# Sixteen of the 22 row blocks of a down projection by seven block products instead of eight, on one Trainium2 core

## The chip, the cores and the metric

The kernel runs on one core of a Trainium2 chip. The metric is the device time of one execution in microseconds (us). Three runs of the kernel before took 1229.63, 1230.88 and 1231.22 us: the median is 1230.88 us. One more execution was profiled; its own time was 1229.33 us, and the span of its trace is 1227.6 us. The engines are TensorE (PE: matmuls; PEld: its weight loads), VectorE (DVE), ScalarE (ACT), GpSimd (POOL) and SyncE (SP, which only issues transfers here).

## The reference, cut to what matters

```python
x = x + merged @ w_o
hn2 = rmsnorm(x, norm2_w)
up, ffn_new = causal_dwconv(hn2 @ w_up, ffn_buf, ffn_conv_w, ffn_conv_b)
x = x + (jax.nn.silu(up[..., :D_FF]) * up[..., D_FF:]) @ w_down
```

This is the end of one decoder layer: 512 prompt tokens (and 16 meta tokens, which the down projection leaves out) and 64 tokens of running sequences, so 576 columns reach the down projection. The model width is 1024, D_FF is 2816: `w_down` has 22 row blocks of 128 rows and 8 column blocks of 128. Everything is float32. Ahead of it stand the other mixers of the layer (an input projection, a pooling mixer, a state-space scan, their merge), which the change touches only with transfers.

## The kernel before, in words

**A product.** Each float32 operand is cut into a rounded part (`wh`, `hi`) and the rest (`wl`, `lo`). `mm3` (lines 119 to 124) issues three matmuls for one 128x128 weight block: wl by hi (L122), wh by hi (L123), wh by lo (L124). The weights stand still, the tokens stream, a result has 128 output features by some 288 tokens. `load_w` loads weights through SP into `wr` (two buffers, L95); `split_w` has ACT write `wh` (L116) and DVE write `wl` (L117), each with two buffers.

**Order.** `run` (L178 on) goes through a list of units. A unit is all matmuls of one column block; after it come its `post` and then the split of the unit two places further on. A scheduler fixes each engine's order when the program is built; then every engine works strictly in order, and an instruction waits on semaphores. Tiles come from pools of a fixed number of buffers, so an instruction can also wait for a buffer.

**The feed-forward stage.** For each of the 22 blocks j there is a gate unit and a value unit of 48 matmuls. `ffn_conv` (L1152 to L1169) takes a result out of PSUM: POOL first writes the state's columns into `ext` (L1156), DVE scales the two halves into it (L1157 to L1159), POOL saves the last columns (L1161), ACT and DVE do the convolution (L1165, L1167). `gate_post` adds the tanh and its product (L1179, L1180); `val_post` multiplies by the gate (DVE, L1190), rounds (ACT, L1194) and leaves the rest to POOL (L1195).

**The down projection** (`down_units`, L1262) runs in two parts. After block 11 come 8 units over row blocks 0 to 11 (two halves of 288 tokens); after block 21 come 8 units over row blocks 12 to 21 (halves of 320 and 256 tokens), between which the finished columns are transposed and scaled for the output (`out_block`, `out_half`, L1227 to L1260). `down_post` (L1220) adds each half to the residual `x2` on DVE.

POOL issues no transfer in the kernel before. The lines that do the products and the sequence of units:

## Time and profile before

| what | value |
|---|---|
| median of three runs | 1230.88 us |
| the profiled execution, its span | 1229.33 us, 1227.6 us |
| PE busy | 1213.3 us, 99% of the span |
| DVE, ACT, POOL busy | 778.6, 554.3, 163.5 us |
| mean granted TensorE clock | 0.997 of full speed |
| moved by DMA | 144.00 MB, mean 117 GB/s |

The span is that of the trace; the execution's own time contains 1.7 us more. Matmuls are pipelined: the duration in a matmul's row is longer than the time to the next one's start, so durations must not be added up; the distance between starts counts. Rows of DVE and ACT overlap a little for the same reason. "Idle before, releaser" names what ended a wait.

### The profile page before, as it was taken

To read this page: it belongs to the slowest core of one execution; us is meant where nothing else is said; L and a number is where in the kernel's file an instruction comes from. 1 tells how busy PE (TensorE), PEld (TensorE's weight loads), DVE (VectorE), ACT (ScalarE), POOL (GpSimd) and SP (SyncE) were. 2 spreads that over 40 slices of the span, in tenths; PEclk is the share of its full clock that TensorE was granted. 3 is DMA by queue.
4 is the path that set the end of the run, shared out by engine and by line. 5 is a ranking of instruction groups with operands and counts; after the bars stand their busy time and mean duration, and the time that the engine had idled before them with its cause. 6 is when DMAs were issued, how large, how long until landed. Compare 5 with 4: busy or idle time off the path is not lost.

```text
span 1227.6 us, 22630 instructions
## 1 busy us (share of the span) xinstructions
PE 1213.3 (99%) x9159; PEld 1176.5 (96%) x9159; DVE 778.6 (63%) x1378; ACT 554.3 (45%) x1167; POOL 163.5 (13%) x323
## 2 busy tenths in 40 slices
PE   9999999999999999999999999999999999999996
PEld 7999999999999999989999999999999999999996
DVE  6785246668997998886643443477666235667634
ACT  6444443555757567655532223443443112433432
POOL 0340000012012013021100001221212000121100
PEclk9999999999999999999999999999999999999998
DMA  7144425653554545664454432123222223222322
GB/s 213 50 137 128 134 89 181 174 161 80 155 146 124 155 135 154 184 168 118 134 154 123 143 131 98 41 91 96 90 70 78 78 86 104 70 69 91 112 70 77
DMA packets 173432, 144.00 MB, mean 117 GB/s; under 512 B 11622, under 2 KB 162830, under 8 KB 173321
## 3 DMA queue, kind: packets, MB, share of 16 engines
q1 hardware_dynamic: 172865, 142.14, 39.5%
q8 instruction: 72, 1.18, 0.4%
q10 hardware_dynamic: 464, 0.42, 0.1%
q14 instruction: 31, 0.25, 0.1%
HBM read 122.43 MB, written 20.34 MB: 116 GB/s over the span
## 4 chain that ended last, share of the span: by engine, by line
PE 94%; DVE 3%; DMA 1%; issue 1%; ACT 1%; POOL 0%; SPq 0%; DVEq 0%; ACTq 0%; POOLq 0%
PE mm L122 28%; PE mm L123 27%; PE mm L124 27%; PE px L765 2%; PE px L827 1%; PE px L787 1%; PE px L796 1%; PE px L749 1%; DMA wr<-in_w_in_dram 1%; PE px L840 1%; DVE wl L117 1%; PE px L880 1%; PE px L739 0%; DVE ext L561 0%; PE px L122 0%
## 5 line engine op out<-in xcount | busy, mean ns | idle before, releaser
L122 PE MATMUL mm<-s,wl 128*128 128x288 f32 (+4 forms) x2512 | 753.1, 300 | 0.6 <-DVE wl L117 0.6
L123 PE MATMUL mm<-s,wh 128*128 128x288 f32 (+4 forms) x2512 | 746.2, 297 | 0.0
L124 PE MATMUL mm<-s,wh 128*128 128x288 f32 (+4 forms) x2256 | 670.7, 297 | 0.0
L122 PEld LDWEIGHTS mm<-s,wl 128*128 128x128 f32 x2512 | 473.4, 188 | 9.2 <-issue 6.5
L123 PEld LDWEIGHTS mm<-s,wh 128*128 128x128 f32 x2512 | 473.1, 188 | 2.9 <-issue 2.4
L124 PEld LDWEIGHTS mm<-s,wh 128*128 128x128 f32 x2256 | 424.1, 188 | 1.4 <-issue 1.4
L117 DVE TENSOR_TENSOR wl<-wr,wh 128x1024 fp32r<-128x1024 f32 (+1 forms) x164 | 198.2, 1208 | 173.1 <-ACT wh L116 172.7
L116 ACT ACTIVATE wh<-wr 128x1024 fp32r<-128x1024 f32 (+1 forms) x164 | 170.1, 1037 | 236.2 <-PE mm L124 199.0
L124 PE MATMUL mm<-t,wh 128*128 128x290 f32 (+1 forms) x256 | 76.0, 297 | 0.0
L1167 DVE SCALAR_TENSOR_TENSOR acc<-ext,ffT,acc 128x592 f32<-128x592 f32 x88 | 74.2, 844 | 1.7 <-ACT acc L1165 0.2
L663 DVE SCALAR_TENSOR_TENSOR acc<-ext,scT,acc 128x616 f32<-128x616 f32 x72 | 63.8, 887 | 0.4
L737 ACT ACTIVATE t<-t,TK 128x128 f32<-128x128 f32 (+1 forms) x160 | 49.0, 385 | 25.5 <-DVE t L735 25.5
L952 POOL TENSOR_TENSOR sqs<-sqs,acc 128x578 f32<-128x578 f32 x19 | 32.2, 1697 | 142.2 <-ACT acc L951 77.3
L124 PEld LDWEIGHTS mm<-t,wh 128*128 128x128 f32 x256 | 48.2, 188 | 0.0
L1194 ACT ACTIVATE s<-ext 128x512 fp32r<-128x512 f32 (+1 forms) x44 | 17.1, 436 | 64.3 <-DVE ext L1190 64.3
L1158 DVE TENSOR_TENSOR ext<-mm,t 128x224 f32<-128x224 f32 x43 | 16.8, 391 | 41.7 <-PE mm L124 41.7
L1195 POOL TENSOR_TENSOR s<-ext,s 128x512 fp32r<-128x512 f32 (+1 forms) x44 | 37.4, 871 | 34.7 <-ACT s L1194 34.7
L1220 DVE TENSOR_TENSOR t<-t,mm 128x288 f32<-128x288 f32 (+2 forms) x30 | 13.6, 452 | 44.1 <-PE mm L124 43.9
L884 ACT ACTIVATE t<-t,spr 128x128 f32<-128x128 f32 x128 | 40.3, 394 | 1.1 <-PE px L827 1.0
L806 POOL TENSOR_TENSOR s<-s,tmp 128x256 f32<-128x256 f32 (+1 forms) x32 | 31.9, 1018 | 66.9 <-DVE tmp L800 59.1
L1165 ACT ACTIVATE acc<-ext,ffT 128x592 f32<-128x592 f32 x44 | 38.2, 870 | 1.6 <-DVE ext L1159 1.6
L1161 POOL COPY t<-ext 128x18 f32<-128x18 f32 x44 | 11.3, 258 | 203.1 <-DVE ext L1159 203.0
(292 smaller groups left out, 1288.0 us busy)
## 6 DMA issues: line engine op xcount, KB each, us to landing
wr<-in_w_in_dram SPq DMA_DIRECT2D x29, 1024.0 KB
wr<-in_w_up_dram SPq DMA_DIRECT2D x22, 1024.0 KB
t<-in_state_ssm_dram SPq DMA_DIRECT2D x32, 256.0 KB
t<-cumD SPq DMA_DIRECT2D x16, 512.0 KB
out_dram<-t SPq DMA_DIRECT2D x32, 256.0 KB
wr<-in_w_ssd_out_dram SPq DMA_DIRECT2D x8, 1024.0 KB
wr<-in_w_down_dram SPq DMA_DIRECT2D x8, 768.0 KB
wr<-in_w_down_dram SPq DMA_DIRECT2D x8, 640.0 KB
```

Source lines behind the costliest of these rows:

```text
L116: S.activation(wh[:, :kb, :n], wr, AF.Copy)
L117: V.tensor_tensor(wl[:, :kb, :n], wr, f(wh[:, :kb, :n]), ALU.subtract)
L122: PE.matmul(o, wl[:, k, :m], hi[:, a:b], start=first, stop=False)
L123: PE.matmul(o, wh[:, k, :m], hi[:, a:b], start=False, stop=False)
L124: PE.matmul(o, wh[:, k, :m], lo[:, a:b], start=False, stop=last)
L663: V.scalar_tensor_tensor(acc[:, 0:616], ext[:, k:k + 616], scT[:, kb, 24 + k:25 + k], acc[:, 0:616], op0=ALU.mult, op1=ALU.add)
L737: S.activation(seg[:q, h, :q], seg[:q, h, :q], AF.Exp, scale=-1.0, bias=sums_[:, h:h + 1])
L884: S.activation(v[:, b], v[:, b], AF.Copy, scale=elS[:, 4 * u + 2 * i + b, 4 * g + j:4 * g + j + 1])
L952: G.tensor_tensor(sums[key], sums[key], t[:, :NA], ALU.add)
L1165: S.activation(acc[:, 0:w], ext[:, 0:w], AF.Identity, scale=ffT[:, kb, 16:17], bias=ffT[:, kb, 19:20])
L1167: V.scalar_tensor_tensor(acc[:, 0:w], ext[:, k:k + w], ffT[:, kb, 16 + k:17 + k], acc[:, 0:w], op0=ALU.mult, op1=ALU.add)
L1195: G.tensor_tensor(l, a, f(h), ALU.subtract)
```

## The change: what it does

Row blocks 0 to 15 are taken in two groups of 8. In a group, the weights are seen as a 2x2 arrangement: A11, A12, A21, A22 (the first index: which half of the 1024 output columns; the second: even or odd row blocks). The gated activations are seen as B11, B12, B21, B22 (even or odd row blocks; which 288 tokens). In place of the 8 products A by B the kernel computes 7, with sums of the A and of the B as operands (the table `SEVEN`). Row blocks 16 to 21 stay as they were, in units of 6 row blocks.

The sums S1 to S4 of weights (1 MB each and group) are built in device memory by transfers: a plain copy, issued by ACT, and then one to three additions into it, issued by POOL (`accum_op=add`). There are 8 copies and 14 additions in all. `held_back` ties each to an earlier weight split, and `placed` spreads them over the merge, the output projection, and the feed-forward with the products in it. Weights of the products come in tiles of four products (`Parts`, 1 MB, four transfers); a unit `Two` is two products of 4 weight blocks and one half each, 24 matmuls. The operands N1, N2, T3, T4 are made by DVE in `val_post`. `seven_post` adds each product to up to three places of `x2`. Also, `rs2` moves to another pool, and `ff_states` two units later.

```diff
-        S.activation(wh[:, :kb, :n], wr, AF.Copy)
-        V.tensor_tensor(wl[:, :kb, :n], wr, f(wh[:, :kb, :n]), ALU.subtract)
+        round_done.append(S.activation(wh[:, :kb, :n], wr, AF.Copy))
+        split_done.append(V.tensor_tensor(wl[:, :kb, :n], wr, f(wh[:, :kb, :n]), ALU.subtract))
...
+    SEVEN = (("A11", "B11"), ("A12", "B21"), ("S4", "B22"), ("S2", "N2"), ("S1", "N1"), ("S3", "T3"), ("A22", "T4"))
...
+            rows = src[k0 * 128:(k0 + 8) * 128, :].rearrange("(k e p) c -> e k p c", e=2, p=128)
+            self.at = {f"A{i + 1}{e + 1}": rows[e][:, :, 512 * i:512 * i + 512] for i in range(2) for e in range(2)}
+            self.d = {s: dp.tile([4, 128, 512], F32, name=f"{name}{s}") for s in ("S1", "S2", "S3", "S4")}
...
+            return lambda: held_back(S.dma_start(out=self.d[s], in_=self.at[a]), round_done[-1], mybir.DependencyClass.NoSync)
...
+            return lambda: held_back(G.dma_start(out=self.d[s], in_=self.at[a], accum_op=ALU.add), split_done[-3], mybir.DependencyClass.Sync)
...
+            return [self.copy("S4", "A12"), self.copy("S2", "A11"), self.copy("S1", "A21"), self.copy("S3", "A11")]
...
+            return [self.add("S4", "A11"), self.add("S2", "A21"), self.add("S1", "A22"), self.add("S4", "A21"), self.add("S3", "A21"),
+                    self.add("S2", "A22"), self.add("S4", "A22")]
...
+                self.of = wp.tile([128, 4, 4, 128], F32, tag="wr", bufs=2, name=nm("wr"))
+                for i, v in enumerate(self.views):
+                    DMA.dma_start(out=self.of[:, i], in_=v)
...
+                wh = wp.tile([128, 2, 4, 128], F32R, tag="wh", bufs=WBUFS, name=nm("wh"))
+                wl = wp.tile([128, 2, 4, 128], F32R, tag="wl", bufs=WBUFS, name=nm("wl"))
...
+                    round_done.append(S.activation(wh[:, i, :n], src, AF.Copy))
+                    split_done.append(V.tensor_tensor(wl[:, i, :n], src, f(wh[:, i, :n]), ALU.subtract))
...
+        def product(self, halves=None, piece=None):
+            for (_, _, acts, post), (w, n) in zip(self.prods, self.ws):
+                ps = px_tile()
+                for k in range(n):
+                    act = acts(k)
+                    n2 = act[0].shape[1]
+                    mm3(ps[:, :n2], w, k, 128, act, 0, n2, k == 0, k == n - 1)
+                post(ps)
...
+        split_g(gB[p][0][:, 0:2], gB[p][1][:, 0:2], qd[:, 2:4], G)
+        V.tensor_tensor(n1, qd[:, 0], qd[:, 1], ALU.subtract)
+        V.scalar_tensor_tensor(n2, n1, -1.0, qd[:, 3], op0=ALU.mult, op1=ALU.subtract)
+        V.tensor_tensor(t3, qd[:, 3], qd[:, 1], ALU.subtract)
+        V.scalar_tensor_tensor(t4, n2, -1.0, qd[:, 2], op0=ALU.mult, op1=ALU.subtract)
+        split_g(gB[p][0][:, 2:4], gB[p][1][:, 2:4], t[:, 0:2 * NH].rearrange("p (h t) -> p h t", h=2), V)
+        split_g(gB[p][2][:, 1], gB[p][2][:, 3], t3, V)
...
+        if w == "A11":
+            u = held["u"] = acc_tile()[:, :NH]
+            S.activation(u, p, AF.Copy)
+            to(0, p, ALU.add)
+        elif w == "S2":
+            u = held["u"]
+            V.tensor_tensor(u, u, p, ALU.add)
+            to(2, u, ALU.subtract)
+        elif w == "S1":
+            u = held.pop("u")
+            V.tensor_tensor(u, u, p, ALU.add)
+            to(1, u, ALU.add)
+            to(3, u, ALU.subtract)
+        elif w == "S3":
+            to(2, p, ALU.subtract)
+            to(3, p, ALU.subtract)
...
-    up = ff_units(0, 12)
+    up = ff_units(0, 8)
...
-    down0 = down_units(0, [6, 6], GHALF)
-    last = down_units(12, [8, 2], LAST)
+    up2, up3 = ff_units(8, 8), ff_units(16, 6)
+    last = down_units([5, 1], LAST)
...
-    seq = up + down0 + ff_units(12, 10) + [out_begin, last[0]]
+    seq = (placed(up, {0: d0.adds()[6:7], 1: d1.copies()[3:4], 4: d1.adds()[0:1], 8: d1.adds()[1:2], 12: d1.adds()[2:3]})
+           + up2[:1] + placed(down_sevens(0), {1: d1.adds()[3:4], 9: d1.adds()[4:5]})
+           + placed(up2[1:], {2: d1.adds()[5:6], 6: d1.adds()[6:7]}) + up3[:1] + down_sevens(1) + up3[1:]
+           + [out_begin, last[0]])
```

**First place: DVE, start of the down projection.** In the program before, DVE's order from the last feed-forward product (L1190) through the first three units of the down projection; L117 splits weights, L1220 adds a result to `x2` (`t`):

```order
L1190 TENSOR_TENSOR ext_10723<-ext_10723,acc_10801 128x8x8
L117 TENSOR_TENSOR wl_10814<-wr_10811,wh_10813 128x768 [waits DMAHW6_49,Activation_49]
L1220 TENSOR_TENSOR t_7478<-t_7478,mm_10821 128x288 [waits PE_49]
L1220 TENSOR_TENSOR t_7478<-t_7478,mm_10822 128x288 [waits PE_49]
L117 TENSOR_TENSOR wl_10818<-wr_10811,wh_10817 128x768 [waits Activation_49]
L117 TENSOR_TENSOR wl_10900<-wr_10897,wh_10899 128x768 [waits DMAHW7_49,Activation_49]
L1220 TENSOR_TENSOR t_7478<-t_7478,mm_10907 128x288 [waits PE_49]
L1220 TENSOR_TENSOR t_7478<-t_7478,mm_10908 128x288 [waits PE_49]
```

In the changed program, the same place: the gate unit of block 8 stands between block 7 and the seven products, and its convolution (L1278, L1290) falls among the first weight splits (L250) and additions (L1419 to L1432, `seven_post`):

```order
L250 TENSOR_TENSOR wl_10390<-wr_10313,wh_10389 128x512 [waits DMAHW5_49,Activation_49]
L1278 SCALAR_TENSOR_TENSOR acc_10383<-ext_10377,ffT,acc_10383 128x592 [waits Activation_49]
L1419 TENSOR_TENSOR t_7488<-t_7488,px_10395 128x288 [waits Activation_49]
L1278 SCALAR_TENSOR_TENSOR acc_10383<-ext_10377,ffT,acc_10383 128x592 [waits DVE_49]
L1419 TENSOR_TENSOR t_7488<-t_7488,px_10411 128x288 [waits DVE_49,PE_49]
L250 TENSOR_TENSOR wl_10426<-wr_10318,wh_10425 128x512 [waits DMAHW6_49,Activation_49]
L1290 SCALAR_TENSOR_TENSOR ext_10377<-ext_10377,acc_10383 128x592 [waits Activation_49]
L250 TENSOR_TENSOR wl_10426<-wr_10318,wh_10425 128x512 [waits DMAHW7_49]
L1419 TENSOR_TENSOR t_7488<-t_7488,px_10436 128x288 [waits PE_49]
L1428 TENSOR_TENSOR acc_10408<-acc_10408,px_10450 128x288 [waits PE_49]
L250 TENSOR_TENSOR wl_10466<-wr_10318,wh_10465 128x512 [waits DMAHW0_49,Activation_49]
```

Splits became shorter (512 elements in place of 768) and stand between one to three additions.

**Second place: POOL, in the feed-forward stage.** Before, POOL's order around one value unit (L1156 prepares `ext`, L1161 saves columns, L1195 is the rest of a product):

```order
L1156 COPY ext_9889<-ffT 128x8x2 [waits Pool_49]
L1161 COPY t_8533<-ext_9751 128x18 [waits DVE_49]
L1161 COPY t_8533<-ext_9819 128x18 [waits DVE_49]
L1156 COPY ext_9957<-ffT 128x8x2 [waits DVE_49,Activation_49,Pool_49]
L1195 TENSOR_TENSOR s_9818<-ext_9751,s_9817 128x512 [waits PE_49,Activation_49]
```

In the changed program, POOL's order where two of the additions stand (L203 is an addition into a sum, 512 rows of 512 numbers; L1267 prepares `ext`, L1272 saves columns, L1299 is the rest of an operand):

```order
L1299 TENSOR_TENSOR s_9587<-t_9582,s_9587 128x288 [waits PE_49,Activation_49]
L203 DMA w1S_147<-in_w_down_dram 512x1x512 [waits DMAHW6_49,DVE_49]
L1272 COPY t_8549<-ext_9712 128x18 [waits DVE_49]
L1299 TENSOR_TENSOR s_9586<-t_9582,s_9585 128x576 [waits PE_49,Activation_49]
L1272 COPY t_8549<-ext_9792 128x18 [waits DVE_49]
L1267 COPY ext_9859<-ffT 128x8x2 [waits Activation_49,Pool_49]
L1272 COPY t_8549<-ext_9859 128x18 [waits DVE_49]
L1267 COPY ext_9932<-ffT 128x8x2 [waits Pool_49]
L203 DMA w1S_146<-in_w_down_dram 512x1x512 [waits DMAHW1_49,DVE_49]
```

The next copies into `ext` now stand behind a transfer that POOL issues.

## Rows read from the trace of the kernel before

**Rows 1.** The page, parts 1 and 4: busy time per engine; the chain by engine.

```profile
PE 1213.3 (99%) x9159; PEld 1176.5 (96%) x9159; DVE 778.6 (63%) x1378; ACT 554.3 (45%) x1167; POOL 163.5 (13%) x323
...
PE 94%; DVE 3%; DMA 1%; issue 1%; ACT 1%; POOL 0%; SPq 0%; DVEq 0%; ACTq 0%; POOLq 0%
```

**Rows 2.** Waits of PE: engine, line, for what; us in total, times, longest.

```profile
PE px L880 <- DVE hT L803: 1.8, 3, 0.9
...
PE mm L122 <- DVE wl L117: 0.6, 2, 0.4
```

**Rows 3.** Stretches: feed-forward, then down projection; busy by engine, clock, DMA share, GB/s.

```profile
915.00:935.00 20.00, 20.00 (x152) 20.00 (x151) 14.12 (x24) 7.69 (x10) 2.55 (x7) 1.00 0.15 43
955.00:975.00 20.00, 20.00 (x153) 20.00 (x153) 6.11 (x9) 3.38 (x4) 0.00 (x0) 1.00 0.27 79
```

**Rows 4.** Timeline of DVE, down projection: start, us, line, [idle before, releaser].

```profile
960.73 0.46 DVE L1220 TENSOR_TENSOR t<-t,mm 128x288 f32<-128x288 f32 x1 [0.55 <-PE mm L124]
...
970.28 0.45 DVE L1220 TENSOR_TENSOR t<-t,mm 128x288 f32<-128x288 f32 x1 [0.55 <-PE mm L124]
...
973.54 0.96 DVE L117 TENSOR_TENSOR wl<-wr,wh 128x768 fp32r<-128x768 f32 x1 [0.42 <-ACT wh L116]
```

**Rows 5.** Groups of instructions by line and shape: busy, mean ns; idle before.

```profile
L122 PE MATMUL mm<-s,wl 128*128 128x288 f32 x1048 | 309.8, 296 | 0.0
...
L117 DVE TENSOR_TENSOR wl<-wr,wh 128x768 fp32r<-128x768 f32 x16 | 15.6, 978 | 28.0 <-ACT wh L116 28.0
...
L1190 DVE TENSOR_TENSOR ext<-ext,acc 128x512 f32<-128x512 f32 x22 | 15.0, 682 | 0.1
...
L116 ACT ACTIVATE wh<-wr 128x768 fp32r<-128x768 f32 x16 | 13.5, 845 | 53.8 <-PE mm L124 53.8
...
L1220 DVE TENSOR_TENSOR t<-t,mm 128x288 f32<-128x288 f32 x16 | 7.3, 454 | 19.0 <-PE mm L124 18.8
```

**Rows 6.** Instructions on the tile wr: ns min/median/max, starts, forms.

```profile
L95 SPq DMA_DIRECT2D wr<-in_w_down_dram x16: 367/368/518, 927.1 to 1183.6; - x16
L116 ACT ACTIVATE s<-wr x9: 399/417/420, 16.7 to 1189.8; 128x256 fp32r<-128x256 f32 x9
L117 DVE TENSOR_TENSOR s<-wr,s x9: 408/425/1173, 19.8 to 1190.2; 128x256 fp32r<-128x256 f32 x9
```

**Rows 7.** Timeline of SP: two issues of a load, merged with the wait between.

```profile
984.08 9.91 SPq L95 DMA_DIRECT2D wr<-in_w_down_dram  x2
```

**Rows 8.** Stretches of 0.5 us around the first of these loads (768 KB).

```profile
985.00:985.50 0.50, 0.50 (x6) 0.50 (x5) 0.00 (x0) 0.00 (x0) 0.00 (x0) 1.00 0.26 78
...
986.00:986.50 0.50, 0.50 (x6) 0.50 (x5) 0.00 (x0) 0.00 (x0) 0.00 (x0) 1.00 1.10 291
...
988.00:988.50 0.50, 0.50 (x6) 0.50 (x5) 0.50 (x1) 0.00 (x0) 0.00 (x0) 1.00 0.40 96
```

**Rows 9.** Timeline of POOL, feed-forward stage.

```profile
925.67 0.20 POOL L1156 COPY ext<-ffT 128x16 f32<-128x16 f32 x1
...
938.48 1.02 POOL L1156 COPY ext<-ffT 128x16 f32<-128x16 f32 x1
```

**Rows 10.** Timeline of DVE, the same stage.

```profile
924.78 0.39 DVE L1158 TENSOR_TENSOR ext<-mm,t 128x224 f32<-128x224 f32 x1 [1.37 <-PE mm L124]
925.09 0.22 DVE L1159 TENSOR_TENSOR ext<-mm,t 128x64 f32<-128x64 f32 x1
...
928.63 0.45 DVE L1157 TENSOR_TENSOR ext<-mm,t 128x290 f32<-128x290 f32 x1
...
931.19 0.39 DVE L1158 TENSOR_TENSOR ext<-mm,t 128x224 f32<-128x224 f32 x1 [0.85 <-PE mm L124]
...
938.48 0.96 DVE L117 TENSOR_TENSOR wl<-wr,wh 128x768 fp32r<-128x768 f32 x1 [0.36 <-ACT wh L116]
```

**Rows 11.** Timeline of DVE at the end.

```profile
1213.16 1.67 DVE L1254 TENSOR_SCALAR s<-s,rf 128x512 f32<-128x512 f32 x4
...
1217.66 0.42 DVE L1220 TENSOR_TENSOR t<-t,mm 128x256 f32<-128x256 f32 x1 [2.50 <-PE mm L124]
```

More of the change, by code (lines that the diff above doesn't have):

```diff
@@ new lines, in seven_units @@
+    def seven_units(sums, mps, acts, post):
+        todo = [(mp, w, x) for mp in mps for w, x in SEVEN]
+        parts = [Parts([sums.view(w, mp) for mp, w, _ in todo[i:i + 4]]) for i in range(0, len(todo), 4)]
+        for a, b in zip(parts, parts[1:]):
+            a.nxt = b
+        prods = [(parts[i // 4], i % 4, lambda k, x=x: acts(k)[x], lambda ps, mp=mp, w=w: post(mp, w, ps))
+                 for i, (mp, w, x) in enumerate(todo)]
+        return [Two(prods[i:i + 2]) for i in range(0, len(prods), 2)]
@@ L209, in weave, with placed @@
         return out + steps[done:]
+    def placed(units, steps):
+        return [x for i, u in enumerate(units) for x in [u, *steps.get(i, ())]]
     def pairs(n, dt, new=big):
@@ L983, in y_split @@
             yn.append((blk(yh, i), blk(yl, i)))
+    d0, d1 = (Sums(w_dn_m, 8 * i, f"w{i}") for i in range(2))
     EARLY = ((0, 256), (256, 592))
@@ L1065, in hybrid_step @@
     seq += [lambda: conv_states(), z[12], z[13], lambda: y_split(0), z[14], lambda: y_split(1), z[15], lambda: y_split(2),
-            gb[5], gb[6], gb[7], lambda: y_split(3)]
+            gb[5], d0.copies()[0], gb[6], d0.copies()[1], gb[7], lambda: y_split(3)]
     mh, ml = [], []
@@ L1138, in hybrid_step @@
     o_units[0].k_outer = True
-    run(merge[:2] + [ff_params] + merge[2:] + [lambda: xr.extend(load_x(c) for c in range(5))], o_units)
-    x2s = []
+    m0, m1 = placed(merge[:2], {0: [*d0.adds()[0:1], d0.copies()[2]], 1: d0.copies()[3:4]}), placed(merge[2:], {0: d0.adds()[1:2], 2: d0.adds()[2:3], 4: d0.adds()[3:4]})
+    run(m0 + [ff_params] + m1 + [lambda: xr.extend(load_x(c) for c in range(5))], o_units)
+    x2s, rs2 = [], []
     def x2_norm():
-        return rnorm(sums["n2"], DM, lambda r, a, b: S.activation(rs2[:, a:b], r, AF.Copy))
-    nff, rs2 = slot([128, 18 * 44]), slot([128, NA])
+        spread = rnorm(sums["n2"], DM, lambda r, a, b: S.activation(rs2[0][:, a:b], r, AF.Copy))
+        rs2.append(ep.tile([128, NA], F32, tag="sqs", bufs=1, name=nm("sqs")))
+        return spread
+    nff = slot([128, 18 * 44])
     LF = LP - A0
@@ new lines, in val_post @@
+        if e == 0:
+            quad[p] = slot([128, 4, NH])
+        qd = quad[p]
+        g = qd[:, 2 * e:2 * e + 2].rearrange("p h t -> p (h t)")
+        for o, a, b in zip((g[:, 0:NP], g[:, NP:].rearrange("p (b j) -> p b j", b=NB)), parts(t), parts(acc)):
+            V.tensor_tensor(o, a, b, ALU.mult)
+        if e == 0:
+            new = slot if p % 4 == 3 else big
+            gB[p] = [new([128, 4, NH], F32R), new([128, 4, NH], F32R), big([128, 4, NH], F32R),
+                     gB[p - 1][3] if p % 2 else big([128, 4, NH], F32R)]
+            split_g(gB[p][2][:, 0], gB[p][2][:, 2], qd[:, 0], G)
+            return
@@ L1260, in out_half, with seven_post, to, down_sevens @@
                 S.dma_start(out=o_ys.rearrange("b j d -> (b j) d"), in_=y[q:n, :])
-    def down_units(j0, kbs, halves):
-        return mat_units(w_dn_m, j0, kbs, 1, lambda: [(blk(gh, j0 + k), blk(gl, j0 + k)) for k in range(sum(kbs))], halves,
+    held = {}
+    def seven_post(mp, w, ps):
+        def to(c, src, op):
+            o = blk(x2, mp + 4 * (c // 2))[:, NMETA + NH * (c % 2):NMETA + NH * (c % 2) + NH]
+            V.tensor_tensor(o, o, src, op)
+        p = ps[:, :NH]
+        if w == "A11":
[14 more added lines that the diff above has]
+            to(3, p, ALU.subtract)
+        else:
+            c = {"A22": 2, "S4": 1, "A12": 0}[w]
+            to(c, p, ALU.subtract if c == 2 else ALU.add)
+    def down_sevens(i):
+        return seven_units((d0, d1)[i], range(4), lambda k: g_ops(4 * i + k), seven_post)
+    def down_units(kbs, halves):
+        return mat_units(w_dn_m, 16, kbs, 1, lambda: [(blk(gh, k), blk(gl, k)) for k in range(6)], halves,
                          lambda m, pss: down_post(m, halves, pss))
-    up = ff_units(0, 12)
+    up = ff_units(0, 8)
     x_turn(0)
-    run(o_units, up)
+    run(placed(o_units, {0: d0.adds()[4:5], 1: d1.copies()[0:1], 3: d1.copies()[1:2], 4: d0.adds()[5:6], 6: d1.copies()[2:3]}), up)
     x2s += [(blk(x2h, k), blk(x2l, k)) for k in range(KD)]
```

93 lines of the change are left out of this document (75 added, 18 removed).

## The prediction

> **What bounds the kernel now.** I read the page first: PE is busy 99% of the span and makes up 94% of the chain that ended last [rows 1]. Then the waits of PE: none exceeds 1.8 us in total, and for a split of weights it waits 0.6 us in all [rows 2]. So the matmuls set the time, one after the other, and the other engines count only where they would make PE wait. Then two stretches: in the down projection PE is busy throughout while DVE works 6.1 of 20 us; in the feed-forward stage DVE works 14.1 of 20 [rows 3]. The reader is to see that the clock stands at 1.00, its upper level of 2.4 GHz, in both.
>
> What a matmul costs must be read from the distance of starts. DVE adds the first half of each unit at 960.73 and 970.28; each time it had waited for PE [rows 4]. So 9.55 us pass per unit of 12 row blocks x 2 halves x 3 = 72 matmuls: 0.1326 us each. The matmul's own row says 296 ns [rows 5], more than twice that; priced by it, the change would seem to be worth 28 us.
>
> **The change part by part.**
>
> *Removed: matmuls.* Before: 12 row blocks x 8 columns x 2 halves x 3 = 576 and 10 x 8 x 2 x 3 = 480, together 1056, at 288 tokens on average. After: 2 groups x 4 column pairs x 7 products x 4 blocks x 3 = 672, and 6 x 8 x 2 x 3 = 288, together 960. That is 96 fewer: 96 x 0.1326 = 12.7 us off the path. Nothing else on PE changes.
>
> *Added: DVE's work within the seven products.* For each of the 8 column pairs PE has 84 matmuls, 11.1 us. DVE has 7 splits of 512 elements and 11 additions of 288. A split of 256 takes 0.425 us [rows 6], of 768 0.978 [rows 5]: 0.70 between them. An addition takes 0.454 [rows 5]. 7 x 0.70 + 11 x 0.454 = 9.9 us. Rows back to back overlap: L1158 starts at 924.78 for 0.39, L1159 already at 925.09 [rows 10], 0.08 before its end. With 18 x 0.08 off that is 8.5 us. So DVE is 76 to 89% occupied, and PE still sets the pace. ACT has 7 splits at 0.63 (0.417 for 256 and 0.845 for 768 [rows 5, 6]) and a copy, under 5 us. Bounds: 0 if DVE always keeps up; at the far end, each split first waits 0.42 us for ACT, as one did [rows 4], and nothing fills it: 9.9 + 7 x 0.42 = 12.8, 1.7 us above PE for each pair, 14 us in all. I take 1.0 us, since the additions fill such waits and five PSUM buffers let them lag.
>
> *Added: the way in.* After the last value unit of a group DVE still has its convolution (2 x 0.85), the product, the four combinations (288 each, at most 0.454), their three rests and two splits, some 8 us, and then the convolution of the gate unit that stands between. The cover is that gate unit: 48 matmuls, 6.4 us, and POOL's operand B21 is first needed one product (1.6 us) later. DVE's order mixes the gate's convolution with the splits of the second and third unit, and by adding up its rows the third unit's first split comes out within 0.1 us of when PE wants it. Two entries at 0.25 us: 0.5 us. Without the cover each entry could cost 4 us.
>
> *Added: operands in the feed-forward stage.* For each pair of blocks, four combinations and rests of 576, 288 and 288 on DVE: 6 x 0.454 + 0.75 (between 0.682 for 512 [rows 5] and 0.978 for 768) = 3.5 us in 25.6 us of PE. DVE goes from 18.1 (14.12 of 20 [rows 3]) to 21.6 us, 84%. It waited for PE before, and a PSUM half has until the next unit's second half: nothing. Its far end is a gate or value result late by the 3.5 us once in a pair, still inside the 6.4 us of a unit.
>
> *Added: loads.* A tile of four products is 1 MB, wanted every 6.4 us. A 768 KB load issued at 984.08 [rows 7] moved its first data after 985.0 and its last before 988.5, at 291 GB/s in between [rows 8]: some 4.1 us, 1.1 of them until the first data and 3.0 of flow; 1 MB so takes 1.1 + 4.0 = 5.1 us. It can start when the tile before last is split, some 6 us before it is wanted, and its first product's quarter is enough for the first split. Nothing alone; beside an addition's traffic the first quarter may double to some 5 us. I take 0.3 us for the two additions that fall there, far ends 0 and 4.
>
> *Added: 8 copies on ACT.* An issue of the same size costs SP 0.37 us [rows 6]; ACT is busy 3.4 to 7.7 of 20 us in the stretches shown [rows 3]. Their traffic falls into the merge stage beside loads that are one tile ahead. 0.2 us; far end 2.
>
> *Added: 14 additions on POOL.* The trace shows none. One must at least be issued: 0.37 us [rows 6]. At the far end POOL is held until the transfer is through: it reads two operands and writes one, 3 MB at the 291 GB/s of [rows 8], 10.8 us, plus 1.1 us to the first data: 12 us. What waits behind it is the next copy into `ext` (L1267). In the trace that copy runs at 925.67 [rows 9], DVE uses it at 928.63, and that may slip to the second half of the next unit: PE ended the unit at 931.1 (DVE waited for it until 931.19 [rows 10]), and 24 more matmuls at 0.1326 are 3.2 us, so 934.3. The slack is 8.6 us. I take the low end, since an issue is all that a queue's engine did in rows 6: nothing, as 8.6 us hide it. The additions into one sum stand 25 us and more apart, so none should wait for the one before.
>
> The Trainium skill says in "DMA: Bandwidth & Descriptors", section "SWDGE vs HWDGE vs iDMA", that an accumulating transfer can only be issued from GpSimd, where software writes every descriptor; the page's fit of 2.0 us plus bytes over 436 GB/s would give, as an estimate, 4.4 us for 1 MB. Held that long POOL would still be inside the slack, and the sum would stay; no run here shows it yet.
>
> *The end.* The second half's last units shrink from 60 to 36 matmuls. Before, DVE was through with scaling the first half at 1214.83 and waited for PE until 1217.66 [rows 11]. The last pair of columns has 24 matmuls of 256 tokens fewer there, 24 x 0.118 (0.1326 by 256/288) = 2.8 us, so PE is done by 1214.85, just when DVE comes free: 0 to 0.5 us are not gained. I take 0.2.
>
> *Sum:* -12.7 + 1.0 + 0.5 + 0.3 + 0.2 + 0.2 = -10.5 us. From the profiled execution's 1229.33 us (its span and 1.7 us around it): 1218.8 us. The median of the runs shown is 1.55 above that execution: 1220.4, I say 1220.5 us.
>
> **The rivals.**
>
> *POOL is held by its additions* (the other side). Six of the 14 stand in the feed-forward stage ahead of copies into `ext`. If POOL is held for X us, PE loses X - 8.6 at each. At the far end, X = 12, that is 6 x 3.4 = 20 us: 1220.5 + 20 = 1241 us. It decides from X = 10.4 on, where 6 x 1.8 eats the 10.5 us. For it: no row shows what such an issue costs, and POOL's queue is in order. Against it: the issues that are shown take 0.37 us and do not wait for their data.
> The Trainium skill has a rule on its side, in "SBUF — State Buffer", section "Who interferes with whom": a DVE instruction with two SBUF inputs holds up a GpSimd instruction that reads SBUF. The trace agrees: a copy that else takes 0.20 us took 1.02 at 938.48, beside a split from 938.48 to 939.44 [rows 9, 10]. DVE gets more of such rows.
>
> *DVE paces the seven products.* For it: up to 89% by its rows, in a fixed order with waits for PE, ACT and itself between. Against it: the overlap of rows. Price, at its far end: 14 in place of 1.0 us, so 1220.5 + 13 = 1233.5 us; at half of it 1227.
>
> *Transfers are late.* The loads of the products, 1.84 MB per 11.1 us (165 GB/s), meet the additions, and the copies meet the loads of the merge. For it: rows of 128 numbers, and three times the traffic for an addition. Against it: DMA shares of 0.15 to 0.27 in these stages [rows 3]. Price: the far ends, 4 + 2 - 0.5 = 5.5 us: 1226 us.
>
> *Nothing is lost:* -12.7, 1218 us.
>
> **How the numbers follow.** Forecast, with the case that nothing is lost: 0.64, own range 1217 to 1224. Transfers late: 0.13. DVE paces: 0.12, spread from 1225 to 1233.5. POOL held: 0.11, nearly all of it above 1231. A measurement of this kernel can tell about 0.2% from no change: from 1228.4 to 1233.3 it would read as none. Faster: 0.64 + 0.13 + 0.05 (of DVE) = 0.82. Within: 0.05 (DVE) + 0.02 (POOL) = 0.07. Slower: 0.02 + 0.09 = 0.11. The range from 1217 to 1231 leaves out 0.10 of the held POOL, 0.05 of DVE and 0.03 below.
>
> **What would show it.** The changed profile should show 96 fewer matmuls, each unit of two products taking 3.2 us, PE at 99%, waits of PE for DVE's splits (L250) of a few us, and DVE at about 80% within the products. POOL's rows behind an addition (L1267) show whether it was held: a gap over 8 us, and PE waiting for PSUM that DVE frees. Wrong it would be if a column pair takes 12 us or more, if ACT's splits wait for transfers, or if the clock falls below its upper level after PE has waited.

## The result, and the profile after

The changed kernel takes 1335.93 us (median of 4 runs, 1334.31 to 1339.61) against 1230.69 us before (4 runs): a ratio of 1.0862, 95% interval 1.0846 to 1.0878. 1220.5 us was forecast. The profiled execution has a span of 1332.8 us, 105.2 more than before.

The page after, parts 1, 3 and 4 (busy time per engine; one DMA queue: packets, MB, share of 16 engines; the chain by engine), answers to [rows 1]:

```profile
PE 1230.6 (92%) x9063; PEld 1187.7 (89%) x9063; DVE 851.6 (64%) x1546; ACT 578.7 (43%) x1223; POOL 205.1 (15%) x321
...
q0 software_dynamic: 28896, 14.85, 7.0%
...
PE 72%; DMA 14%; DVE 10%; ACT 2%; issue 1%; SPq 0%; POOL 0%; DVEq 0%; ACTq 0%; POOLq 0%
```

There are 96 PE instructions fewer, as forecast. But PE is idle for 1332.8 - 1230.6 = 102.2 us, before for 14.3. Its busy time has grown by 17.3 us although 12.7 us of matmuls are gone, so the rest takes 30.0 us more: 87.9 + 30.0 - 12.7 = 105.2. Most of those 30.0 us are the clock: taken us by us over the trace, 53 us of PE's busy time lie at the granted clock's lower level, half of the upper one, which costs some 27 us; the other 3 are not explained. DMA, 1% of the chain before, is 14% now. Queue q0 is GpSimd's and holds the 14 additions.

The waits of PE (for what; us in total, times, longest), against 0.6 us for a split in [rows 2]:

```profile
PE mm L122 <- DVE wl L117: 28.4, 11, 11.3
PE px L1206 <- DMA s<-in_ffn_conv_w_dram: 19.0, 1, 19.0
PE px L1225 <- DMA t<-in_x_prompt_dram: 14.5, 3, 10.9
PE px L122 <- DVE wl L250: 12.7, 5, 4.3
PE mm L122 <- DVE ext L1268: 11.8, 4, 5.7
```

Two of these name a transfer. Behind the splits (L117, L250) stands one too, as ACT's waits show. Behind L1268 stands a split that came late: here ACT waits for a load, DVE's split (L117) follows from 931.32 to 932.55, and then L1268.

```profile
ACT wh L116 <- DMA wr<-in_w_up_dram: 71.7, 12, 14.0
```

```profile
930.23 1.06 ACT L116 ACTIVATE wh<-wr 128x1024 fp32r<-128x1024 f32 x1 [11.41 <-DMA wr<-in_w_up_dram]
...
932.46 0.45 DVE L1268 TENSOR_TENSOR ext<-mm,sqs 128x290 f32<-128x290 f32 x1
```

Two stretches of seven products, the first beside an addition, the second with none left (columns as in [rows 3]):

```profile
995.00:1015.00 20.00, 10.29 (x40) 9.63 (x41) 6.09 (x13) 4.08 (x7) 0.00 (x0) 0.62 0.41 96
1175.00:1195.00 20.00, 20.00 (x153) 20.00 (x152) 16.41 (x34) 7.84 (x15) 0.00 (x0) 1.00 0.68 195
```

In the second PE issues 153 matmuls in 20 us at the upper clock, as before the change; in the first 40, and by the mean of 0.62 three quarters of the time at the lower level of 1.2 GHz, to which the clock fell after PE had stood still. The work of the two is of the same kind; the transfers beside it differ. This is how long POOL spends on an addition, and how long it takes to land (instructions on L203; ns min/median/max):

```profile
L203 POOL DMA_DIRECT2D w0S<-in_w_down_dram x7: 1900/1908/2070, 643.0 to 838.4; - x7
L203 POOL DMA_DIRECT2D w1S<-in_w_down_dram x7: 1906/1907/1932, 870.6 to 1088.6; - x7
...
DMA to landing us min/median/max: 25.4/29.3/31.6
```

POOL is held for 1.9 us, but the transfer lives for 29. Now one of them: POOL's timeline, and a piece of the chain (start, us, what):

```profile
982.38 1.91 POOL L203 DMA_DIRECT2D w1S<-in_w_down_dram  x1 [5.06 <-DMA wr<-w0S]
```

```profile
985.27 24.38 DMA wr<-in_w_down_dram
```

A load of the products (a quarter of a tile, 256 KB), under way from 2.9 us after the addition's start, ends the wait 24.38 us later. Before, a load of 768 KB needed some 4.1 us [rows 7, 8]. And yet the DMA engines were not busy on average. The same 2 us of that wait, by engine with clock, DMA share and GB/s, and then by queue:

```profile
996.00:998.00 2.00, 0.66 (x3) 0.66 (x4) 0.69 (x1) 0.56 (x1) 0.00 (x0) 0.61 0.29 55
```

```profile
q0 software_dynamic: 43, 0.09, 23.6%
q1 hardware_dynamic: 41, 0.02, 5.3%
```

The addition takes 23.6% of 16 engines: the work of 3.8 engines. The share alone does not tell whether four engines are full or sixteen a quarter full. The packets of the trace do: from 982 to 1013 us three or four of the addition's packets are under way at once in three quarters of its time. So some four engines are full, and most of the others stand idle while PE waits.

### The profile page after: what moved, and what is told of

The parts are those of the page before. It is cut to its first block, busy times and chain, and to the rows that moved or that the text cites. A ratio compares the mean times of both kernels' runs of the same rounds, so it can differ in the third digit from the quotient of the medians.

```text
span 1332.8 us, 22868 instructions
## 1 busy us (share of the span) xinstructions
PE 1230.6 (92%) x9063; PEld 1187.7 (89%) x9063; DVE 851.6 (64%) x1546; ACT 578.7 (43%) x1223; POOL 205.1 (15%) x321
## 3 DMA queue, kind: packets, MB, share of 16 engines
q0 software_dynamic: 28896, 14.85, 7.0%
## 4 chain that ended last, share of the span: by engine, by line
PE 72%; DMA 14%; DVE 10%; ACT 2%; issue 1%; SPq 0%; POOL 0%; DVEq 0%; ACTq 0%; POOLq 0%
PE mm L122 19%; PE mm L123 19%; PE mm L124 19%; DMA wr<-in_w_up_dram 8%; DVE wl L117 2%; DMA t<-in_x_prompt_dram 2%; DMA s<-in_state_ffn_dram 2%; PE px L122 2%; DMA wr<-in_w_down_dram 2%; PE px L123 2%; PE px L124 2%; PE px L871 1%; DVE acc L1278 1%; PE px L933 1%; PE px L893 1%
## 5 line engine op out<-in xcount | busy, mean ns | idle before, releaser
L122 PE MATMUL mm<-s,wl 128*128 128x290 f32 (+4 forms) x2278 | 693.6, 304 | 40.2 <-DVE wl L117 28.4
L123 PE MATMUL mm<-s,wh 128*128 128x290 f32 (+4 forms) x2278 | 685.1, 301 | 0.0
L124 PE MATMUL mm<-s,wh 128*128 128x290 f32 (+3 forms) x2022 | 606.5, 300 | 0.0
L122 PEld LDWEIGHTS mm<-s,wl 128*128 128x128 f32 x2278 | 437.1, 192 | 51.8 <-issue 27.5
L123 PEld LDWEIGHTS mm<-s,wh 128*128 128x128 f32 x2278 | 436.9, 192 | 2.9 <-issue 2.4
L124 PEld LDWEIGHTS mm<-s,wh 128*128 128x128 f32 x2022 | 385.6, 191 | 1.4 <-issue 1.4
L117 DVE TENSOR_TENSOR wl<-wr,wh 128x1024 fp32r<-128x1024 f32 (+1 forms) x148 | 181.2, 1226 | 189.3 <-ACT wh L116 189.3
L116 ACT ACTIVATE wh<-wr 128x1024 fp32r<-128x1024 f32 (+1 forms) x148 | 153.4, 1039 | 236.2 <-PE mm L124 143.0
L122 PE MATMUL px<-s,wl 128*128 128x288 f32 (+4 forms) x234 | 72.8, 311 | 13.8 <-DVE wl L250 12.7
L1278 DVE SCALAR_TENSOR_TENSOR acc<-ext,ffT,acc 128x592 f32<-128x592 f32 x88 | 73.4, 847 | 1.0 <-ACT acc L1276 0.2
L124 PE MATMUL px<-s,wh 128*128 128x288 f32 (+4 forms) x234 | 71.8, 307 | 0.0
L123 PE MATMUL px<-s,wh 128*128 128x288 f32 (+4 forms) x234 | 71.5, 306 | 0.0
L122 PEld LDWEIGHTS px<-s,wl 128*128 128x128 f32 x234 | 46.1, 197 | 15.8 <-DVE wl L250 14.5
L249 ACT ACTIVATE wh<-wr 128x512 fp32r<-128x512 f32 x56 | 32.5, 624 | 49.7 <-PE px L124 21.4
L1272 POOL COPY t<-ext 128x18 f32<-128x18 f32 x44 | 24.5, 558 | 182.9 <-DVE ext L1270 169.2
L250 DVE TENSOR_TENSOR wl<-wr,wh 128x512 fp32r<-128x512 f32 x56 | 36.7, 685 | 19.4 <-ACT wh L249 19.0
```

Source lines behind the costliest of these rows:

```text
L116: round_done.append(S.activation(wh[:, :kb, :n], wr, AF.Copy))
L117: split_done.append(V.tensor_tensor(wl[:, :kb, :n], wr, f(wh[:, :kb, :n]), ALU.subtract))
L122: PE.matmul(o, wl[:, k, :m], hi[:, a:b], start=first, stop=False)
L123: PE.matmul(o, wh[:, k, :m], hi[:, a:b], start=False, stop=False)
L124: PE.matmul(o, wh[:, k, :m], lo[:, a:b], start=False, stop=last)
L249: round_done.append(S.activation(wh[:, i, :n], src, AF.Copy))
```

## The experiments

**First: is it the additions, their kind, or their bytes?** Additions left out:

```diff
-            return lambda: held_back(G.dma_start(out=self.d[s], in_=self.at[a], accum_op=ALU.add), split_done[-3], mybir.DependencyClass.Sync)
+            return lambda: None
```

Expected: 

> The 14 additions are left out, so S1 to S4 hold only what was copied into them; copies, product loads, splits, matmuls and the order of everything else stay. Theory: an accumulating transfer of 1 MB takes 25 to 32 us and every load beside it is late by up to that much. Then with the additions gone the 105 us go: 1217 to 1224 us, the forecast's own range. Rival A, the seven products themselves (DVE's additions and splits, tiles of four products): at least 1300 us stay. Rival B, the traffic as such (copies and 1.84 MB of loads per column pair): the 14 additions are 42 of some 87 MB that the change moves (3 MB each, copies 2 MB each, products 29.4 MB), so about half of the loss stays: 1275 us.

Measured: 1238.39 us (ratio 1.0069, 1.0056 to 1.0083). Without the additions 97.5 us are gone, part of it by another order of the engines (at least 48 of DVE's 1546 instructions stand elsewhere in the trace). But some 18 us above the forecast remain that no side had expected.

Plain copies from GpSimd:

```diff
-            return lambda: held_back(G.dma_start(out=self.d[s], in_=self.at[a], accum_op=ALU.add), split_done[-3], mybir.DependencyClass.Sync)
+            return lambda: held_back(G.dma_start(out=self.d[s], in_=self.at[a]), split_done[-3], mybir.DependencyClass.Sync)
```

Expected: 

> Each of the 14 additions becomes a plain copy of the same 1 MB into the same place, from the same queue of GpSimd at the same time, so the sums are wrong; only the accumulation is gone. Theory, that it is the accumulation (read, add and write back): a copy lands in under 12 us and the time falls to 1219 to 1230 us. Rival A, that it is GpSimd's software queue: copies still land after 25 us and more, 1320 to 1340 us. Rival B, bytes: 2 of 3 MB remain, 1285 to 1300 us.

Measured: 1274.04 us (1.0366, 1.0350 to 1.0381). Landing:

```profile
DMA to landing us min/median/max: 13.1/14.5/17.8
```

All three expectations missed. The copies land in 14.5 us, half the time, and of the 115 us above the forecast some 54 are left, so the accumulation is not the whole cause. The order of all engines, PE too, is that of the changed kernel here, so the 62 us that are gone belong to the accumulation alone.

Plain copies from ScalarE (`add` returns what `copy` does):

```diff
+            return self.copy(s, a)
```

Expected: 

> The 14 additions become plain copies of the same 1 MB issued by ScalarE as the 8 others are, so the sums are wrong. Theory of the accumulation: 1219 to 1230 us, like the plain copies from GpSimd. Rival A, GpSimd's software queue: 1219 to 1230 us here, but 1320 or more with the plain copies from GpSimd. Rival B, bytes: 1285 to 1300 us here too.

Measured: 1302.55 us (1.0584, 1.0564 to 1.0603), a little above all that was expected. The scheduler's order had changed with it (at least 82 of DVE's instructions stand elsewhere), so it tells little by itself.

Sums made, but not read:

```diff
-            full = self.d[name] if name in self.d else self.at[name]
+            full = self.at[{"S1": "A12", "S2": "A21", "S3": "A22", "S4": "A11"}.get(name, name)]
```

Expected: 

> Copies and additions stay, but the products load blocks of the weight itself in place of S1 to S4 (so the result is wrong): nothing waits for a finished sum any more. Theory, that the additions hold up other transfers: the loss stays, 1320 to 1340 us. Rival C, that the loss comes from product loads that wait until a sum is finished: it goes, 1220 to 1230 us.

Measured: 1335.13 us, in one run, with the order of PE, DVE, ACT and POOL unchanged. Nobody waits for a finished sum; the additions harm as bystanders.

**Second: few engines.** In copies without accumulation, and from either queue, the trace showed long tails of 100 GB/s at a share of 0.27. The transfers are written `[4, 128, 512]`; the new theory was that 4 outermost means 4 engines.

```diff
+    def rows_out_first(ap):
+        return ap.rearrange("k p c -> p k c")
...
-            return lambda: held_back(S.dma_start(out=self.d[s], in_=self.at[a]), round_done[-1], mybir.DependencyClass.NoSync)
+            return lambda: held_back(S.dma_start(out=rows_out_first(self.d[s]), in_=rows_out_first(self.at[a])), round_done[-1], mybir.DependencyClass.NoSync)
...
-            return lambda: held_back(G.dma_start(out=self.d[s], in_=self.at[a], accum_op=ALU.add), split_done[-3], mybir.DependencyClass.Sync)
+            return lambda: held_back(G.dma_start(out=rows_out_first(self.d[s]), in_=rows_out_first(self.at[a]), accum_op=ALU.add), split_done[-3], mybir.DependencyClass.Sync)
```

Rows outermost in all. Expected: 

> All copies and additions stay and the result is the same; only the order of dimensions in which each transfer is written down changes, from 4 blocks x 128 rows x 512 to 128 rows x 4 blocks x 512. New theory: a transfer with 4 outermost runs on few of the 16 DMA engines (after a copy's first us the trace shows 100 GB/s at a DMA share of 0.27, about 4 engines of 16), and a load issued beside it, spread over all, has to wait for its parts on those. Then with 128 outermost an addition lands in 8 to 12 us in place of 29, the waits of PE fall to a few us, and the time is 1222 to 1245 us. Rival, that accumulation or device memory as the target is slow by itself: additions still land after 25 us, and the time stays at 1320 to 1340 us.

Measured: 1223.99 us (0.9956, 0.9942 to 0.9970): a little faster than before. The landing, and q0 on the page:

```profile
DMA to landing us min/median/max: 8.6/9.7/14.7
```

```profile
q0 software_dynamic: 7392, 14.68, 7.1%
```

An addition's work has stayed: 7.0% x 16 x 1332.8 / 14 = 107 us of one engine then, 7.1% x 16 x 1223.3 / 14 = 99 now. It is spread otherwise: 107 / 29.3 = 3.6 engines on average, 99 / 9.7 = 10.2 now. A plain copy in the old form has 49 (3.4% of q0) over 14.5 us: 3.4 engines. So accumulating doubles the work, and four engines in place of sixteen trebles the time.

Copies with rows outermost as above, and the additions left out as in the first kernel. Expected: 

> The 14 additions are left out (the sums are wrong) and the 8 copies are written with the 128 rows outermost. Theory of the few engines: the stalls in the merge beside the copies go, and of the 1238.4 us with the old order of dimensions 12 to 17 us go: 1221 to 1226 us. Rival, that the copies' bytes cost: 1236 to 1240 us.

Measured: 1220.43 us (0.9921, 0.9907 to 0.9934). Of the 18 us nothing is left; and the additions, in this form and the same order of DVE and ACT, cost 3.6 us together.

Neither copies nor additions, sums not read:

```diff
-            return lambda: held_back(S.dma_start(out=self.d[s], in_=self.at[a]), round_done[-1], mybir.DependencyClass.NoSync)
+            return lambda: None
```

Expected: 

> Neither copies nor additions run, and the products load blocks of the weight itself in place of S1 to S4 (so the result is wrong): what is left is seven products, their loads and DVE's work. Theory, that transfers from device memory to device memory are the whole loss: the forecast without its terms for copies and additions, 1220.5 - 0.5 = 1220 us, in 1217 to 1224. Rival, that products and operands cost more than forecast: 1230 us or more, since with the additions alone left out 1238.4 us were measured.

Measured: 1220.30 us (0.9922, 0.9908 to 0.9935). The forecast without its two terms for transfers was 1220. The terms left for products and operands (-12.7 + 1.0 + 0.5 + 0.2) make a gain of 11.0 us; against the kernel before in the same set of runs (1229.99 us) it was 9.7. So they were priced rightly within 1.3 us; that the time itself is met within 0.3 us is in part luck, since the kernel before ran 0.9 us faster in this set than in the one the forecast started from.

**Third: does the outermost number set the engines?** Eight copies of 1 MB in one kernel, cut by q = 16, 8, 4, 2, 32, 64, 128 and 4 (the code is cut):

```diff
+            gap = dp.tile([q, r + 1, 512], F32, name=f"gap{i}")
+            S_dma = S.dma_start(out=gap[:, :r, :], in_=w_dn_m[2048:2560, 0:512].rearrange("(q r) c -> q r c", q=q))
```

Expected: 

> Nothing makes sums and the products load blocks of the weight itself (so the result is wrong); in the feed-forward stage stand 8 plain copies of 1 MB (512 rows of 2 KB), issued by ScalarE some 19 us or more apart, each into a place with a gap behind every q-th part, so that q stays the outermost number: q = 16, 8, 4, 2, 32, then 64, 128, 4. Theory, that q engines work, 16 at most: where a copy runs alone, q = 2 shows 50 GB/s and a DMA share of 0.13, q = 4 100 GB/s and 0.27, q = 8 200 GB/s and 0.5, 16 and above 300 GB/s or more and a share over 0.8; the time is 1221 to 1235 us. Rival, that the two orders differ for another reason (where the rows lie in memory): all eight run alike, at the same share within 0.1.

Measured: the rates as expected. These are stretches in which only a copy moves, q = 16, 8, 4, 2 and 128 (the last two columns are DMA share and GB/s):

```profile
806.00:807.00 1.00, 1.00 (x10) 1.00 (x9) 1.00 (x4) 0.97 (x2) 0.37 (x2) 1.00 1.03 395
829.00:830.00 1.00, 1.00 (x10) 1.00 (x9) 1.00 (x3) 0.00 (x0) 0.00 (x0) 1.00 0.52 199
853.00:854.00 1.00, 1.00 (x10) 1.00 (x9) 0.97 (x4) 0.82 (x2) 0.00 (x0) 1.00 0.27 104
885.00:886.00 1.00, 1.00 (x10) 1.00 (x9) 0.00 (x0) 0.00 (x0) 0.00 (x0) 1.00 0.13 51
1018.00:1020.00 2.00, 2.00 (x18) 2.00 (x17) 1.97 (x4) 0.00 (x0) 0.20 (x1) 1.00 0.99 377
```

That is some 25 GB/s for each engine, and q engines, 16 at most. The packets say the same. A copy has 512 rows, and its queue shows 512 + q packets: 528, 520, 516 and 514 for q = 16, 8, 4 and 2, and 528 again for 32, 64 and 128, as if each engine added one. The first and the last of these four:

```profile
q10 hardware_dynamic: 528, 1.05, 13.8%
...
q10 hardware_dynamic: 514, 1.05, 10.7%
```

A load beside the copy of q = 8, by queue in 834 to 837 us (q10 is the copy):

```profile
q1 hardware_dynamic: 365, 0.37, 34.9%
q10 hardware_dynamic: 95, 0.18, 15.9%
```

Together that is 51%, the work of eight engines. It fits that the load's parts on the other eight are through and that it waits for those on the engines that it shares with the copy: in the trace the copy ends at 836 and the load a good 1 us later. So a load can be late by about as long as the slow transfer lasts. The time, 1254.64 us in one run, missed its expectation: PE also stood where nothing was moving at all, behind a full DVE queue:

```profile
861.00:866.00 5.00, 0.00 (x0) 0.00 (x0) 4.96 (x6) 2.51 (x3) 2.61 (x3) 0.73 0.00 0
```

So there is a second effect. At least 57 of DVE's instructions stand elsewhere than with the products alone: other transfers, another order. That the scheduler reckons with transfer times when it orders the engines is the likely reason.

Copies in pieces of 4 x 32 rows and of 8 x 16 rows, meant as the same question, were no test of it: each piece ran on all 16 engines, presumably because rows that follow each other are taken as one dimension, 128 rows x 512, in both. The packets show it: queue q10 has 4688 in the whole run with 8 copies on 16 engines, and 384 more, 24 x 16, with 32 pieces:

```profile
q10 hardware_dynamic: 4688, 8.81, 2.2%
...
q10 hardware_dynamic: 5072, 8.81, 2.3%
```

The edits, cut:

```diff
+                for k in range(4):
+                    o, i = (x[k].rearrange("(q p) c -> q p c", q=4) for x in (self.d[s], self.at[a]))
...
+                    o, i = (x[k].rearrange("(q p) c -> q p c", q=8) for x in (self.d[s], self.at[a]))
```

Expected: 

> The 14 additions are left out (the sums are wrong); each of the 8 copies is issued as 4 copies of 256 KB, each with 4 outermost (4 x 32 rows x 512). Theory, that the outermost number sets how many of the 16 engines work: still 4 engines, so the stretch of a copy shows about 100 GB/s at a DMA share near 0.27, and the loss of the copies stays: 1234 to 1240 us (1238.4 with whole copies of 4 outermost, 1220.4 with 128 outermost). Rival, that one transfer of 1 MB is too long to stand beside a load: with pieces of 256 KB the loss falls to a quarter, 1222 to 1227 us.

And: 

> The 14 additions are left out (the sums are wrong); each of the 8 copies is issued as 4 copies of 256 KB, each with 8 outermost (8 x 16 rows x 512). Theory: 8 engines, so a copy alone moves at about 200 GB/s and a share near 0.5 and is through in half the time; a load is late by half as much, most of it inside the lead of a load: 1221 to 1229 us. Rival of the too long transfer: the same time as with pieces of 4 outermost, within 2 us.

Measured: 1242.39 and 1242.90 us, alike, and the trace shows no slow tail: a piece moves at up to 262 GB/s. The theory of the engines has no reason for those 22 us above 1220.43, and the rival expected less too. In ACT's timeline the pieces are spread through its work, and a split (L116) comes behind them, though the load that it needs had moved its last data by 826:

```profile
827.05 0.50 ACTq L203 DMA_DIRECT2D w1S<-in_w_down_dram  x1
...
832.22 0.50 ACTq L203 DMA_DIRECT2D w1S<-in_w_down_dram  x1
...
833.55 1.04 ACT L116 ACTIVATE wh<-wr 128x1024 fp32r<-128x1024 f32 x1
```

**Fourth: engines or order?** Writing the rows outermost had moved at least 66 instructions of DVE, 40 of ACT and 26 of POOL. So I crossed the two: the form of the transfers from one kernel, the order of DVE, ACT, POOL and SP from the other, fixed by order-only dependencies. PE's order was not fixed. In the traces its matmuls stand in almost the same order in all of these kernels, but the transposes of the convolution's weights (L1206) and of `x_prompt` (L1225), which wait for loads, stand elsewhere among them.

```diff
+        for a, b in zip(names, names[1:]):
+            tc.add_manual_dep(made[f"I-{b}"], f"I-{a}", mybir.DependencyInfo(mybir.DependencyClass.NoSync, mybir.DependencyReason.DATA),
+                              reason="order of the other kernel")
```

Slow form, other order. Expected: 

> The transfers of the changed kernel (4 outermost) with the instructions of DVE, ScalarE, GpSimd and SyncE in the order that the scheduler gave them where the rows stand outermost (1223.99 us); the result is the same. Theory, that the slow transfers do the harm by themselves: 1320 to 1345 us. Rival, that the harm is the order into which the scheduler put the engines because it reckons with slow transfers: 1222 to 1230 us. Both, half and half: 1270 to 1300 us.

Full spread, old order. Expected: 

> Rows outermost in all copies and additions, but the four engines in the order of the changed kernel (1335.93 us); the result is the same. Theory of the slow transfers: 1222 to 1230 us. Rival of the order: 1320 to 1345 us. Half and half: 1260 to 1290 us.

The same without additions. Expected: 

> Additions left out (the sums are wrong), copies with 4 outermost (1238.39 us in their own order), engines in the order of the kernel whose copies have the rows outermost (1220.43 us). Theory of the slow transfers: 1236 to 1240 us; rival of the order: 1219 to 1222 us. I lean to the rival here: in the run with 1238.39 us ScalarE's waits for a transfer of w_up came to 9.8 us, and in the merge no load was waited for.

And: 

> Additions left out (the sums are wrong), copies with the rows outermost, engines in the order that took 1238.39 us. Theory of the slow transfers: 1219 to 1222 us; rival of the order: 1236 to 1240 us.

Measured (us, median):

| | old order | other order |
|---|---|---|
| copies and additions, 4 outermost | 1335.93 | 1332.70 |
| copies and additions, rows outermost | 1246.41 | 1223.99 |
| copies alone, 4 outermost | 1238.39 | 1226.17 |
| copies alone, rows outermost | 1233.68 | 1220.43 |

With additions the form is worth 89.5 us in the old order and 108.7 in the other; the order 22.4 us where transfers are quick, 3.2 where they are slow. Some of what is called form here may be the place of PE's transposes: their waits for transfers come to 33.5 us in the changed kernel, to 42.3 in the crossed one with the slow form and to 0.8 in the one with the quick form. The rest of PE's waits and the clock do not hang on them. So the theory of the slow transfers held for the slow form in the other order (1320 to 1345) and missed the quick form in the old order (1222 to 1230) by the order's part. With copies alone both theories missed, since both causes are there: the order weighs 12 to 13 us, the form 5 to 6. The waits of PE in the crossed pair, slow form first, then quick form in the old order:

```profile
PE mm L122 <- DVE wl L117: 35.4, 9, 12.1
PE px L1206 <- DMA s<-in_ffn_conv_w_dram: 24.0, 1, 24.0
```

```profile
PE mm L122 <- DVE wl L117: 9.6, 6, 2.8
PE mm L122 <- DVE ext L1271: 6.1, 3, 2.5
```

With the quick form PE waits for a transfer for 0.8 us in all (`x_prompt`); what remains above that is DVE coming late in an order made for slow transfers.

**Two versions that might beat both.** Sums by GpSimd in SBUF, from the four blocks of each column pair, without any transfer inside device memory:

```diff
+                s1, s2, s4 = (tmp_tile((128, 4, 128)) for _ in range(3))
+                for o, a, b in ((s1, a21, a22), (s2, s1, a11), (s4, s2, a12), (a21, a21, a11)):
+                    G.tensor_tensor(o, a, b, ALU.add)
```

Expected: 

> No transfer makes sums: for each column pair the four blocks A11, A12, A21, A22 are loaded (1 MB), and GpSimd makes S1 to S4 in SBUF with four additions of 512 elements, a pair ahead. Theory, that only the transfers from device memory to device memory went wrong: the seven products keep their gain, 1219 to 1225 us. Rival: GpSimd's additions hold up DVE's rows or come late, some 5 us per column pair at worst, 1235 to 1260 us.

Measured: 1232.95 us (1.0026, 1.0015 to 1.0036); between the theory and the rival, and slower than before. GpSimd's sums, DVE's splits from 895 to 935 us, and the same splits without the sums beside them (groups by shape: busy, mean ns | idle):

```profile
L234 POOL TENSOR_TENSOR tmp<-tmp,wr 128x512 f32<-128x512 f32 x16 | 26.8, 1676 | 2.9 <-POOL tmp L234 1.4 <-DMA wr<-in_w_down_dram 1.1
```

```profile
L263 DVE TENSOR_TENSOR wl<-wr,wh 128x512 fp32r<-128x512 f32 x11 | 10.9, 1014 | 0.0
```

```profile
L249 DVE TENSOR_TENSOR wl<-wr,wh 128x512 fp32r<-128x512 f32 x23 | 15.1, 684 | 0.7 <-ACT wh L248 0.6
```

The 1014 ns, in place of 684, mix splits with and without an addition beside them. Over the whole run (ns min/median/max):

```profile
L263 DVE TENSOR_TENSOR wl<-wr,wh x32: 674/685/1783, 896.2 to 1101.7; 128x512 fp32r<-128x512 f32 x32
```

Counted from the trace, of the 56 splits of the products the 35 with no addition beside them take 683 ns on average, at most 694; the 21 with one take 1330. And DVE was the engine with the least room.

Then the version with rows outermost (1223.99 us). Of its 3.7 us above the products alone, most lie at one place. POOL's timeline, a piece of the chain, and the stretch after it:

```profile
933.68 1.25 POOL L206 DMA_DIRECT2D w1S<-in_w_down_dram  x1 [23.26 <-DVE wl L253]
```

```profile
936.57 9.96 DMA wr<-in_w_up_dram
```

```profile
949.00:953.00 4.00, 3.90 (x18) 3.93 (x19) 2.27 (x4) 1.06 (x1) 0.00 (x0) 0.57 0.03 7
```

One load beside one addition is some 5 us late, PE waits for 2.0 us and then runs at the lower clock for 3. So the additions among the products were placed elsewhere:

```diff
-... 4: d1.adds()[0:1], 8: d1.adds()[1:2], 12: d1.adds()[2:3]})
-           + up2[:1] + placed(down_sevens(0), {1: d1.adds()[3:4], 9: d1.adds()[4:5]})
-           + placed(up2[1:], {2: d1.adds()[5:6], 6: d1.adds()[6:7]}) + up3[:1]
+... 2: d1.adds()[0:1], 5: d1.adds()[1:2], 8: d1.adds()[2:3], 11: d1.adds()[3:4]})
+           + up2[:1] + down_sevens(0)
+           + placed(up2[1:], {1: d1.adds()[4:5], 4: d1.adds()[5:6], 7: d1.adds()[6:7]}) + up3[:1]
```

Expected: 

> All copies and additions with the 128 rows outermost, as in the version that took 1223.99 us, and the two additions of the second group that stood among the first group's products are issued elsewhere: one in the feed-forward units before, one in those behind. Theory: of that version's 3.7 us above the products alone (1220.3 us), most belong to one load of w_up that took 9.96 us beside an addition issued 2.9 us before it, after which PE waited 2.0 us and ran 3 us at the lower clock; with no addition there the time is 1220 to 1222 us. Rival, that the additions cost their 3.7 us wherever they stand: 1223 to 1225 us.

Measured: 1221.06 us (0.9928, 0.9915 to 0.9942), with DVE and ACT in the same order. It beats both kernels.

## Why the prediction was wrong

*The step that failed* is the term for loads beside additions, "I take 0.3 us for the two additions that fall there, far ends 0 and 4", and with it the rival "Transfers are late", priced at 5.5 us. Measured, with everything in place: some 90 to 109 us by the form of the transfers, and 3 to 22 us by the order. Three things were wrong in it.

First, the price of an addition. Its far end was 3 MB at the 291 GB/s of [rows 8], 12 us; it took 29.3. The 291 GB/s were read from a load whose outermost number is 128. A transfer with 4 outermost was taken to flow likewise. It moves 100 GB/s as a plain copy and half of that when it adds. Nor does a run show the 4.4 us that the prediction estimated for 1 MB: an addition landed after 29.3 us, and after 9.7 us with the rows outermost.

The Trainium skill has this rule on a page that the prediction cited for another: "DMA: Bandwidth & Descriptors", section "Why a DMA increments its semaphore by 16 and not by 1", says that a transfer runs on the largest number of engines up to 16 that divides the slowest dimension of both its sides. The trace of the kernel with eight copies agrees: shares of 0.13, 0.27, 0.52 and about 1 for q of 2, 4, 8 and 16. By that rule and the `[4, 128, 512]` of the change, an addition would have been seen as a matter of four engines beforehand.

Second, the argument against that rival: "DMA shares of 0.15 to 0.27 in these stages" [rows 3]. The share is a mean over 16 engines. A load is through when its last engine is, so four crowded engines are enough to delay it, and the mean stays low: 0.29 while PE was busy for 0.66 of 2 us.

Third, where the additions stand. Only the two among the products were counted; the other twelve stand beside loads of `w_up`, `w_o`, `x_prompt` and the convolution's weights, and those made most of the waits. The text did name what followed: "if the clock falls below its upper level after PE has waited". That came, and is some 27 of the 117.9 us that were lost (87.9 of waiting and 30.0 of slower work).

*The copies* were priced at 0.2 us, far end 2. With rows outermost they cost 0.1 us (1220.43 - 1220.30); as written 18 us (1238.39 - 1220.43), of which the crossed runs give about two thirds to the order. That the scheduler would reorder DVE and ACT because of a transfer's form was not thought of.

*What was right.* The 96 matmuls. DVE within the products: 76 to 89% was forecast, the second group shows 16.41 of 20, 82%, and PE does not wait; so the rival that DVE paces is out here (in the version with GpSimd's sums, where DVE is busy for 19.9 of the 20 us from 895 and PE for 16.3, it came true). The way in: without transfers PE waited 1.1 us in all for splits of the products, 0.5 forecast. POOL is held for 1.9 us, inside the 8.6 us of slack, and in the trace no engine waits for the copy into `ext` (L1267): that rival was wrong. With the products alone the sum was 1220 us and the measurement 1220.30.

```profile
PE px L122 <- DVE wl L249: 1.1, 2, 0.6
```

*What stays open.* Why plain copies from ScalarE cost more (1302.55 us) than from GpSimd (1274.04): the order differs too, and they were not crossed. In pieces of 256 KB the order explains the 22 us only by likeness, and not all of them: the old order gave 13 us with whole copies (1233.68 - 1220.43). And how much of the form's part is PE's transposes standing in front of late loads was not measured by itself.

## What to carry to other kernels

Read the outermost number of every transfer before pricing it: here 2, 4 and 8 kept a copy on 2, 4 and 8 engines, and loads beside such a transfer were late by up to as long as it lasted. A low DMA share is no proof of room; divide it by the engines that the transfer can use, and ask which load shares them. Where a scheduler orders the engines, compare the order too before a difference between two kernels is put down to the one line that was edited; crossing form and order separates the two, best with the order of every engine fixed.
